# Low weight parts of a first block by ScalarE's negative copy and an accumulating DMA, in place of VectorE's subtraction

## The chip, the cores and the metric

The kernel runs on one core of a Trainium2 chip. The core has five engines with a queue of instructions each, which run in order: TensorE (PE), VectorE (DVE), ScalarE (ACT), GpSimd (POOL) and SyncE (SP). Sixteen DMA engines move data between the HBM and the on-chip memory (SBUF). The metric is device time in microseconds. Before the change the median of two runs is 3559.07 us (3555.22 and 3562.92).

## The reference

Two blocks are computed one after the other, on 512 latent tokens (and 256 context tokens in block 1) of width 2048, all in fp32. Block 1 is one hybrid layer:

```python
u_l = rms_norm(h_lat, pre_w) * (1 + scale_l[:, None]) + shift_l[:, None]
u_c = rms_norm(h_ctx, pre_w) * (1 + scale_c) + shift_c
z_l, xbc_l, dt_l, qkv_l, b_l, a_l = _split_proj(u_l @ w_in)
z_c, xbc_c, dt_c, qkv_c, b_c, a_c = _split_proj(u_c @ w_in)
...
ssd_c, ssd_l = ssd_mixer(xbc_c, dt_c, xbc_l, dt_l, ssd_a_log, ssd_dt_bias, ssd_d)
gdn_c, gdn_l = gdn_mixer(qkv_c, b_c, a_c, qkv_l, b_l, a_l, gdn_a_log, gdn_dt_bias)
...
h_lat = h_lat + gate_l[:, None] * merge(ssd_l, gdn_l, z_l, h_lat.dtype)
```

`scale`, `shift` and `gate` come from a modulation, a vector times a 2048 x 6144 matrix. `ssd_mixer` is a state-space scan, `gdn_mixer` a gated delta rule with a triangular solve in each chunk of 128 tokens; both run forward and backward. `merge` norms both halves, gates them with `silu(z)`, multiplies by `w_out` and norms again. Block 2 has two layers of its own (HGRN2 and RG-LRU, then mLSTM), each with an input projection, an output projection and a gated embedding. The change doesn't reach it.

## The kernel before

Every large product is an fp32 product made of three faster ones. Each operand is split into a high part (the value rounded to the fp32r format of PE) and a low part (the value less its high part), and a product is low x high + high x low + high x high. The parts of the activations (`xh`, `xl`) are made once and stay in SBUF; the parts of the weights are made for each tile, just ahead of their use.

`gemm_steps` (L165) is the line of the products. A weight block is 2048 x 128 and comes in four tiles of 128 partitions x 4 chunks x 128 columns, 256 KB each. For each tile SP loads the raw weights `wr` (L180, four buffers), ScalarE copies them into the high part `wh` (L183), and VectorE subtracts to get the low part `wl` (L184). `wh` and `wl` have six buffers each (`w_bufs`). Then 12 matmuls a stream follow (L198), for each of the four chunks first the one with the low weight part. The three steps of the weights are traced with high priority. Some blocks run over the latent tokens alone (`lat`, 512 columns), others over latent and context (`both`, 512 and 256).

Block 1 goes through these stages:

- Startup (`startup`, L309): 16 steps of the modulation. In each, 2 MB of `wada` come in eight tiles, ScalarE makes the high part (L336), VectorE the low part of six tiles and GpSimd that of two (L337), PE multiplies (L340); then the activations of one contraction chunk are normed, modulated and split (`modulate`, L367). The first four blocks of weights (`w_xbc`, `w_small`) are multiplied chunk by chunk beside it.
- Phase A (`phase_a`, L760): first the SSD, with its blocks of x, B and C, its units of four heads and the first k and v blocks; then the preparation of the gated delta rule, `gdn_prep` (L658) for eight heads, each with loads of decays (`E`, `Rgb`), a first step on GpSimd (L671), transposes and products on PE, stores, and two solves on GpSimd for heads 0 to 3 (`gdn_solve`, L738, L752 and L754).
- Phase B (`phase_b`, L1079): the scans of eight heads, with the remaining 21 blocks (z and queries) woven between the dependent matmuls. PE's order is written out by hand here (`run_slots`, `feed`); the first head's loads are put ahead of the weights on SP.
- `merge` (L1239): output projection, norm, gate, residual.

The startup and phase A are laid out by a planner that simulates the engines (`schedule_with_timeline_sim`, L1898); each engine then keeps the order that it was given. In all, block 1 takes 53 weight blocks ahead of `merge`: 12 of `w_xbc`, 1 of `w_small`, 24 of `w_qkv`, 16 of `w_z`.

Of the kernel before, what the change touches and what calls it, by code (L numbers as in the profile page):

```python
# [17 lines left out]
# products of other blocks between the dependent ones of the gated delta rule, by weight  # L18
# [4 lines left out]
# ---------------------------------------------------------------- layout on the host  # L23
# [107 lines left out]
# ---------------------------------------------------------------- the program  # L131
class Prog:
# [8 lines left out]
    # ---- constants  # L141
# [18 lines left out]
    # ---- products with split operands  # L160
# [4 lines left out]
    def gemm_steps(self, blocks, kc=16):  # L165
        """blocks: dicts of src [128, kc, M], acts [(hi, lo, psum ap)], done().  The blocks run
        together, contraction chunk by contraction chunk; a step is one matmul."""
# [6 lines left out]
        for q in (self.order if kc == 16 else range(kc // qk)):  # L174
            sp = []
            for b in blocks:
                m = b["src"].shape[2]
                with self.tc.high_priority():
                    r = wp.tile([P, qk, m], F32, tag="wr", name="wr", bufs=self.wr_bufs)
                    nc.sync.dma_start(r, b["src"][:, q * qk:(q + 1) * qk, :])  # L180
                    hi = wp.tile([P, qk, m], F32R, tag="wh", name="wh", bufs=self.w_bufs)
                    lo = wp.tile([P, qk, m], F32R, tag="wl", name="wl", bufs=self.w_bufs)
                    nc.scalar.activation(out=hi, in_=r, func=AF.Copy)  # L183
                    nc.vector.tensor_tensor(out=lo, in0=r, in1=hi.bitcast(F32), op=SUB)  # L184
                sp.append((hi, lo))
# [18 lines left out]
    def gemm_tokens(self, src, done):  # L204
        """A product with the tokens in the partitions: src [128, 16, n], done(chunk of tokens, psum)."""
# [22 lines left out]
    def weave(self, steps, n, weight):  # L228
        """Steps of other products to place between dependent matmuls: n of them over the given weight."""
# [11 lines left out]
    def run_slots(self, chain, other=None, skip=0, scale=1.0):  # L241
        """A chain of dependent products; between two of them a link of the other chain and steps of the filler."""
# [24 lines left out]
    # ---- small helpers  # L267
# [13 lines left out]
    def rsqrt_rows(self, acc, n, out, tmp):  # L281
        """out[p, t] = (sum_p acc[p, t] / n + eps) ** -0.5, the same in every partition."""
# [6 lines left out]
        # one table for both  # L289
# [3 lines left out]
        # one step of Newton's method  # L293
# [4 lines left out]
    def transposes(self, ps, dst, srcs):  # L298
        """PE transposes of srcs (each [a, b]) next to each other into one bank, one copy out."""
# [8 lines left out]
    # ---- block 1, phase A: modulation, input projections of both streams, SSD, GDN preparation  # L308
    def startup(self):  # L309
        nc, D = self.nc, self.D  # L310
        self.xh, self.xl, self.ch, self.cl = [], [], [], []
        with self.tc.tile_pool(name="st", bufs=2, side="right") as st:
# [8 lines left out]
            # both vectors' high and low parts, next to each other as stationary columns  # L321
# [33 lines left out]
            def square(k):  # L355
                # the streams wait in the places of their parts
# [24 lines left out]
            # the first modulations run beside the loads of the streams  # L381
# [13 lines left out]
    def conv_consts(self):  # L395
        """Half of the convolutions' taps and bias: silu(x) = (tanh(x / 2) + 1) * (x / 2)."""
# [22 lines left out]
    def conv5(self, ps, is_lat, taps, bias, out, th):  # L419
        """out = silu of the centred convolution of ps."""  # L420
# [20 lines left out]
    def both(self, src, done, share=None):  # L441
        """A block over the latent tokens and over the context."""
# [10 lines left out]
    def conv_block(self, names, j, has_bias, sink):  # L453
        """done() of a block that goes through a convolution; sink(out_lat, out_ctx)."""
# [16 lines left out]
    def small_done(self, ps, pc):  # L471
        """dt, beta and alpha of all tokens (context first): decays and their sums in each chunk."""
        nc, b1 = self.nc, self.b1
        with self.tc.tile_pool(name="sm", bufs=1, side="right") as st:
# [59 lines left out]
            # decay to the chunk's end times dt; minus the decay from the chunk's start  # L534
# [5 lines left out]
    # ---- SSD: units of four heads  # L540
# [3 lines left out]
    def ssd_bc(self, kind, lat, ctx):  # L544
        """B or C of a group: keep the feature-major latent part, B also token-major."""
# [12 lines left out]
    def to_tm(self, dst, lat, ctx, eng="act"):  # L558
        """dst[:, c, :] (token-major chunks) from feature-major latent and context parts."""
# [19 lines left out]
    def ssd_unit(self, u, xt):  # L579
        """Four heads; xt [tokens of a chunk, chunk, 256] holds their x."""  # L580
# [35 lines left out]
        # feature-major, to DRAM  # L616
# [40 lines left out]
    # ---- gated delta rule, preparation: everything that needs k and v alone  # L657
    def gdn_prep(self, h):  # L658
# [23 lines left out]
        # token-major k and its squared norms  # L682
# [19 lines left out]
        # token-major v over the norm of k  # L702
# [8 lines left out]
        # X[j, i] = k_j . k_i with the decay between j and i: forward above, backward below  # L711
# [9 lines left out]
        # its diagonal blocks of 32, rows scaled, lower triangular for both directions  # L721
# [16 lines left out]
    def gdn_solve(self, h, g, eng):  # L738
        """Inverses of the unit lower triangular 32-blocks of two heads, a block in a partition."""
# [6 lines left out]
        # in place: 2 on the diagonal turns the column of a step into its negative  # L746
# [13 lines left out]
    def phase_a(self):  # L760
# [74 lines left out]
        with tc.tile_pool(name="gp", bufs=1, side="right") as self.gp:  # L835
# [18 lines left out]
            # the first queries and gate, while the last preparations end  # L854
# [13 lines left out]
    # ---- gated delta rule: the inverses, the scans  # L868
    def gdn_data(self, h, hd):
        """What the scans of a head need."""  # L870
# [4 lines left out]
    def gdn_load(self, h):  # L875
        """The operands of the products for a head's inverses."""
# [35 lines left out]
    def gdn_merge(self, hd):  # L912
        """W = (I + D X)^-1 of every chunk (forward: upper, backward: lower), from its diagonal
        blocks; both directions share the products."""
# [11 lines left out]
        # 32 -> 64  # L926
# [13 lines left out]
        # 64 -> 128  # L940
# [17 lines left out]
    def gdn_step(self, h, hd, cs, S, tag, last=False):  # L958
        """One chunk of both directions' scans: the corrected values; the next states into S."""
# [47 lines left out]
    def gdn_lat(self, h, hd, qf, before):  # L1007
        """before: what takes the last head's outputs."""
# [11 lines left out]
        # squared norms of q  # L1020
# [34 lines left out]
        # the norms of q and of the outputs, token by token  # L1055
# [15 lines left out]
    def zgate(self, ps, pool, pin=lambda ins: ins):  # L1071
        """2 silu(z)."""
# [6 lines left out]
    def phase_b(self):  # L1079
        nc, tc, D = self.nc, self.tc, self.D  # L1080
        self.yF = self.dr.tile([16, P, 512], F32, name="yF")
        with (tc.tile_pool(name="cq", bufs=1) as self.cv, tc.tile_pool(name="gq", bufs=1, side="right", reuse_waits="tile") as g):
            self.gq = g
            self.pads_lat(self.cv)
            # places: what comes first where the last phase ends early
# [14 lines left out]
            # parity of the block of 32 rows  # L1100
# [24 lines left out]
            def others():  # L1125
                """The products beside the scans, and what follows from them."""
# [16 lines left out]
            with tc.manual_schedule(engines={E.PE}):  # L1143
                # the first head's loads before the weights
# [14 lines left out]
                for h in range(8):  # L1159
                    # the next head's inverses and context beside the latent tokens' scans  # L1160
# [35 lines left out]
    # ---- the streams between the products  # L1196
    def acts(self, order=(0, 1, 2, 3)):
        """New activations, whose chunks are taken up four by four in this order."""
# [3 lines left out]
    def act(self, k, raw, scale=None):  # L1202
        """Contraction chunk k of the next product, in its two parts."""
# [11 lines left out]
    def stage(self, src, n, done, group=4, extra=(), filler=None):  # L1215
        """A product's blocks: the first ones together, so that they keep up with its input."""
# [21 lines left out]
    # ---- block 1: output projection, norm, gate, residual; the per-layer embeddings  # L1238
    def merge(self):  # L1239
# [4 lines left out]
        with tc.tile_pool(name="mp", bufs=1, side="right") as g:  # L1244
            self.act_from(self.yF, (0, 2, 1, 3))
            self.ple_in(g, 1)
            # gate of the modulation
# [19 lines left out]
            # the stream, in the places of the gate's weights  # L1267
# [7 lines left out]
            # some of the embeddings' products run beside the norm  # L1275
# [16 lines left out]
    # ---- per-layer embeddings: projections, their norms; they wait for nothing  # L1292
# [25 lines left out]
    def norm_rows(self, acc, tmp):  # L1318
        """The norm's scale of each token, and half of it."""
# [4 lines left out]
    def columns(self, Rc):  # L1324
        """The norm's scale of each token as columns."""
# [10 lines left out]
    def silu_rows(self, pool, ps, tag, bufs=2, out=None):  # L1336
        """silu of the normed projection."""
# [22 lines left out]
    # ---- even layer  # L1360
    def even(self):
        nc, tc, D = self.nc, self.tc, self.D
        self.yF = self.dr.tile([16, P, 512], F32, name="yF2")
        with tc.tile_pool(name="ep", bufs=1, side="right") as g:
# [7 lines left out]
            # masks of the levels: s in a first half, t in the second half of the same block; and the other way  # L1372
            self.lm, self.lt = {}, {}
            tmp = g.tile([P, 64], F32, name="lmt")
            for m in (64, 32, 16, 8, 4, 2, 1):
# [3 lines left out]
                # 2 m b <= s < 2 m b + m  # L1379
# [7 lines left out]
                # 2 m b + m <= t < 2 m b + 2 m  # L1387
# [576 lines left out]
```

## Time and profile before

| | |
|---|---|
| median of two runs | 3559.07 us |
| span of the profiled execution | 3565.4 us (its own time is not given beside the span) |
| PE busy | 3410.4 us, 96% |
| VectorE busy | 2172.4 us, 61% |
| ScalarE busy | 1511.4 us, 42% |
| GpSimd busy | 543.6 us, 15% |
| share of the 16 DMA engines (the queue that carries the data) | 45.1% |
| read from HBM | 415.17 MB |

Busy time counts the stretch in which an engine has an instruction running; PE's is modelled from pipelined matmuls. Stages are read best from their own stretch, since each has another limit: startup 0 to 205 us, SSD 205 to 550, preparation 550 to 780, scans 780 to 1205, and from there `merge` and block 2.

### The profile page before, as it was taken

What the parts mean: (1) busy time and instruction counts of PE and PEld (TensorE: products, weight loads), DVE (VectorE), ACT (ScalarE), POOL (GpSimd) and SP (SyncE); (2) the same over time, 40 slices, a digit from 0 to 9 for tenths busy, and PEclk for the clock granted to TensorE, in tenths of its full rate; (3) what the DMA queues carried; (4) which work ended last, traced back from release to release, by engine and by line L of the source; (5) the groups of instructions that cost most, each with busy time, mean ns of one, the idle gap of its engine ahead of it and who ended that gap; (6) DMA issues with size and microseconds to landing.
All of it is one profiled execution on the core that took longest, in us unless ns stands there. A gap on an engine that the chain in (4) does not pass through costs nothing.

```text
span 3565.4 us, 49253 instructions
## 1 busy us (share of the span) xinstructions
PE 3410.4 (96%) x17334; PEld 2843.3 (80%) x17334; DVE 2172.4 (61%) x4187; ACT 1511.4 (42%) x3036; POOL 543.6 (15%) x679
## 2 busy tenths in 40 slices
PE   5899999989999998999999999999999999999998
PEld 4688888878888786778888788887888888878887
DVE  7978776778865657666565634546444535353456
ACT  6554434444444435664333434434333333332334
POOL 4211114851110003202231201000000000000000
PEclk8999999999999999999999999999999999999999
DMA  8723336664443774333323454453333333345345
GB/s 272 239 78 108 92 83 215 205 193 133 126 127 94 231 250 137 101 113 95 98 83 98 116 183 136 136 149 107 107 105 101 101 102 102 89 132 156 96 123 170
DMA packets 293257, 479.79 MB, mean 135 GB/s; under 512 B 53689, under 2 KB 86841, under 8 KB 290833
## 3 DMA queue, kind: packets, MB, share of 16 engines
q1 hardware_dynamic: 293008, 476.65, 45.1%
q8 instruction: 136, 2.23, 0.3%
q14 instruction: 113, 0.92, 0.1%
HBM read 415.17 MB, written 61.34 MB: 134 GB/s over the span
## 4 chain that ended last, share of the span: by engine, by line
PE 72%; DVE 12%; DMA 7%; issue 3%; ACT 3%; POOL 2%; SPq 0%; DVEq 0%; ACTq 0%; POOLq 0%
PE mm L198 52%; PE mm L222 3%; PE mm L223 2%; PE mm L224 2%; PE mmc L198 2%; DVE wl L184 2%; DMA wg<-in_wgate 1%; PE pr L340 1%; DVE e L1570 1%; PE mg L922 1%; PE pl L198 1%; DMA araw<-yF 1%; ACT wh L183 1%; DVE at L1577 1%; PE s L198 1%
## 5 line engine op out<-in xcount | busy, mean ns | idle before, releaser
L198 PE MATMUL mm<-hi,wl 128*128 128x512 f32 (+2 forms) x3632 | 1414.7, 392 | 22.7 <-DVE wl L184 14.6
L198 PE MATMUL mm<-xlo,wh 128*128 128x512 f32 (+2 forms) x3632 | 1421.0, 391 | 6.4 <-DVE xlo L278 6.4
L198 PE MATMUL mm<-hi,wh 128*128 128x512 f32 (+2 forms) x3632 | 1415.1, 390 | 0.0
L184 DVE TENSOR_TENSOR wl<-wr,wh 128x512 fp32r<-128x512 f32 (+1 forms) x940 | 657.4, 705 | 687.0 <-ACT wh L183 683.1
L183 ACT ACTIVATE wh<-wr 128x512 fp32r<-128x512 f32 (+1 forms) x940 | 579.6, 621 | 1153.4 <-PE mm L198 908.0
L198 PEld LDWEIGHTS mm<-hi,wl 128*128 128x128 f32 (+1 forms) x3632 | 687.2, 190 | 149.2 <-DVE wl L184 19.9
L198 PEld LDWEIGHTS mm<-xlo,wh 128*128 128x128 f32 (+1 forms) x3632 | 686.6, 189 | 143.0 <-DVE xlo L278 8.7
L198 PEld LDWEIGHTS mm<-hi,wh 128*128 128x128 f32 (+1 forms) x3632 | 686.0, 189 | 122.8 <-issue 3.6
L222 PE MATMUL mm<-wl,hi 128*128 128x256 f32 (+1 forms) x512 | 172.3, 336 | 0.0
L223 PE MATMUL mm<-wh,xlo 128*128 128x256 f32 (+1 forms) x512 | 172.2, 336 | 0.0
L224 PE MATMUL mm<-wh,hi 128*128 128x256 f32 (+1 forms) x512 | 172.0, 336 | 0.0
L216 ACT ACTIVATE wh<-wr 128x512 fp32r<-128x512 f32 x96 | 60.6, 632 | 156.5 <-PE mm L224 77.7
L217 DVE TENSOR_TENSOR wl<-wr,wh 128x512 fp32r<-128x512 f32 x96 | 68.4, 714 | 88.9 <-ACT wh L216 88.4
L436 DVE SCALAR_TENSOR_TENSOR cvl<-padl,hc,cvl 128x512 f32<-128x512 f32 x112 | 91.8, 827 | 24.7 <-ACT cvl L432 15.5
L198 PE MATMUL mmc<-xlo,wh 128*128 128x256 f32 x368 | 106.0, 288 | 0.0
L222 PEld LDWEIGHTS mm<-wl,hi 128*128 128x128 f32 x512 | 97.2, 190 | 10.4 <-DVE pad L1349 0.3
L198 PE MATMUL mmc<-hi,wl 128*128 128x256 f32 x368 | 105.4, 286 | 0.0
L198 PE MATMUL mmc<-hi,wh 128*128 128x256 f32 x368 | 105.3, 286 | 0.0
L223 PEld LDWEIGHTS mm<-wh,xlo 128*128 128x128 f32 x512 | 97.2, 190 | 10.0
L224 PEld LDWEIGHTS mm<-wh,hi 128*128 128x128 f32 x512 | 97.2, 190 | 10.0
L340 PE MATMUL pr<-wal,c 128*4 128x256 f32 x256 | 69.4, 300 | 23.7 <-DVE c L324 10.6
L336 ACT ACTIVATE wah<-wa 128x512 fp32r<-128x512 f32 x128 | 74.5, 620 | 39.7 <-PE pr L340 23.7
(588 smaller groups left out, 4406.1 us busy)
## 6 DMA issues: line engine op xcount, KB each, us to landing
wr<-in_o_in SPq DMA_DIRECT2D x192, 256.0 KB, 3.1
wr<-in_e_in SPq DMA_DIRECT2D x160, 256.0 KB, 3.1
wr<-in_pgate SPq DMA_DIRECT2D x148, 256.0 KB, 3.3
wa<-in_wada SPq DMA_DIRECT2D x128, 256.0 KB, 4.2
wr<-in_w_qkv SPq DMA_DIRECT2D x96, 256.0 KB, 3.2
wr<-in_w_z SPq DMA_DIRECT2D x64, 256.0 KB, 3.1
wr<-in_w_out SPq DMA_DIRECT2D x64, 256.0 KB, 4.5
wg<-in_wgate SPq DMA_DIRECT2D x16, 1024.0 KB, 7.5
```

Of the source, the lines that this page charges most:

```text
L183: nc.scalar.activation(out=hi, in_=r, func=AF.Copy)
L184: nc.vector.tensor_tensor(out=lo, in0=r, in1=hi.bitcast(F32), op=SUB)
L198: nc.tensor.matmul(ap, w[:, kk, :], x, start=(n == 0), stop=(n == total[key] - 1))
L216: nc.scalar.activation(out=hi, in_=r, func=AF.Copy)
L217: nc.vector.tensor_tensor(out=lo, in0=r, in1=hi.bitcast(F32), op=SUB)
L222: nc.tensor.matmul(ps[c][:, :n], self.xh[k][:, t], lo[:, i], start=first, stop=False)
L223: nc.tensor.matmul(ps[c][:, :n], self.xl[k][:, t], hi[:, i], start=False, stop=False)
L224: nc.tensor.matmul(ps[c][:, :n], self.xh[k][:, t], hi[:, i], start=False, stop=last)
L336: nc.scalar.activation(out=wh, in_=w, func=AF.Copy)
L340: nc.tensor.matmul(pr[0:4, 0:256], c4[:, 2 * q + j, :], x[:, j, :], start=(q + j + i == 0), stop=(q + j + i == 9))
L436: nc.vector.scalar_tensor_tensor(out=ov, in0=pad[:, :, j:j + n], scalar=taps[j], in1=ov, op0=MUL, op1=ADD)
L922: nc.tensor.matmul(v[:, c], lhs[:, c], rhs[:, c], start=True, stop=True)
```

## The change

In `gemm_steps` the low part gets a second way. ScalarE copies the raw weights once more with the scale -1 into the tile of the low part, which rounds and leaves minus the high part there; then a DMA issued by GpSimd reads the same weights from HBM again and adds them to that tile. A switch chooses the way: it is on from the start of `run` and goes off ahead of `merge`.

```diff
                     nc.scalar.activation(out=hi, in_=r, func=AF.Copy)
-                    nc.vector.tensor_tensor(out=lo, in0=r, in1=hi.bitcast(F32), op=SUB)
+                    if self.lo_dma:
+
+                        nc.scalar.activation(out=lo, in_=r, func=AF.Copy, scale=-1.0)
+                        nc.gpsimd.dma_start(lo, b["src"][:, q * qk:(q + 1) * qk, :], accum_op=ADD)
+                    else:
+                        nc.vector.tensor_tensor(out=lo, in0=r, in1=hi.bitcast(F32), op=SUB)
...
         self.wr_bufs, self.w_bufs = 4, 6
+        self.lo_dma = True
         self.order = (0, 1, 2, 3)
...
                 self.pq.release()
                 return
+            self.lo_dma = False
             rp = tc.alloc_tile_pool(name="rp", bufs=1)
```

The rest of the diff takes out comments.

## Rows read from the trace of the kernel before

**Rows 1.** The page's totals: busy us, share of the span, instructions.

```profile
span 3565.4 us, 49253 instructions
PE 3410.4 (96%) x17334; PEld 2843.3 (80%) x17334; DVE 2172.4 (61%) x4187; ACT 1511.4 (42%) x3036; POOL 543.6 (15%) x679
```

**Rows 2.** Windows: us, busy PE, PEld, DVE, ACT, POOL, then clock, DMA share, GB/s.

```profile
0.00:60.00 60.00, 24.51 (x122) 13.43 (x122) 43.31 (x68) 43.66 (x84) 29.19 (x34) 0.80 0.90 305
0.00:205.00 205.00, 157.47 (x959) 116.28 (x960) 166.57 (x286) 124.12 (x242) 68.10 (x70) 0.88 0.69 225
205.00:550.00 345.00, 337.75 (x1943) 296.18 (x1943) 275.40 (x624) 144.22 (x316) 48.27 (x56) 0.99 0.35 95
550.00:780.00 230.00, 211.82 (x1181) 183.51 (x1180) 169.57 (x324) 105.15 (x285) 149.18 (x220) 0.96 0.70 215
600.00:750.00 150.00, 135.60 (x761) 118.01 (x760) 119.51 (x216) 61.97 (x170) 126.90 (x179) 0.95 0.65 201
...
780.00:1205.00 425.00, 403.85 (x2357) 345.61 (x2355) 300.35 (x769) 201.48 (x491) 66.23 (x82) 0.99 0.45 130
1205.00:3565.00 2360.00, 2299.54 (x10900) 1901.74 (x10900) 1260.47 (x2187) 936.41 (x1705) 211.80 (x251) 0.99 0.43 125
```

**Rows 3.** PE's waits by stage: SSD, preparation, scans; us in total, times, longest.

```profile
PE yo L595 <- DVE H L614: 4.8, 2, 2.7
...
PE mm L198 <- DVE wl L184: 1.8, 1, 1.8
...
PE og L1046 <- DVE W L925: 3.9, 6, 0.8
```

**Rows 4.** Waits of all engines over the whole span, the longest total.

```profile
ACT wh L183 <- PE mm L198: 908.0, 452, 12.9
```

**Rows 5.** VectorE's subtraction by stage: ns min/median/max, first and last start us.

```profile
L184 DVE TENSOR_TENSOR wl<-wr,wh x18: 674/679/693, 5.1 to 169.0; 128x512 fp32r<-128x512 f32 x18
L184 DVE TENSOR_TENSOR wl<-wr,wh x71: 674/684/719, 208.1 to 545.1; 128x512 fp32r<-128x512 f32 x71
L184 DVE TENSOR_TENSOR wl<-wr,wh x48: 677/693/2144, 552.2 to 779.7; 128x512 fp32r<-128x512 f32 x48
L184 DVE TENSOR_TENSOR wl<-wr,wh x30: 678/804/2144, 602.2 to 748.2; 128x512 fp32r<-128x512 f32 x30
L184 DVE TENSOR_TENSOR wl<-wr,wh x87: 676/693/1520, 779.7 to 1204.4; 128x512 fp32r<-128x512 f32 x87
```

**Rows 6.** Groups by line, 205 to 1205 us: ScalarE's high copy (busy us, mean ns).

```profile
L183 ACT ACTIVATE wh<-wr 128x512 fp32r<-128x512 f32 x207 | 129.3, 628 | 163.5 <-PE mm L198 89.6 <-PE mmc L198 62.3 <-DMA wr<-in_w_z 4.1
```

**Rows 7.** SP's weight loads (L180): issue in ns, and landing.

```profile
L180 SPq DMA_DIRECT2D wr<-in_w_xbc x48: 327/328/437, 0.8 to 411.9; - x48
...
DMA to landing us min/median/max: 2.0/3.2/9.3
```

**Rows 8.** Groups by line on GpSimd, 600 to 750 us.

```profile
L752 POOL TENSOR_TENSOR To<-T 96x31 f32<-96x31 f32 (+15 forms) x62 | 41.6, 671 | 4.2
L754 POOL TENSOR_TENSOR T<-T,To 96x31 f32<-96x31 f32 (+15 forms) x62 | 41.0, 661 | 4.6
L671 POOL TENSOR_SCALAR E<-E,AAg 128x128 f32<-128x128 f32 x36 | 24.8, 706 | 10.7 <-DMA E<-AA 10.7
...
L678 POOL TENSOR_TENSOR vf<-E,mL 128x512 f32<-128x512 f32 x6 | 8.2, 1363 | 0.1
```

**Rows 9.** The chain at the start of the scans: start us, us, what.

```profile
757.17 6.43 DMA wr<-in_w_z
764.28 0.70 DVE wl L184
```

**Rows 10.** The chain in the startup: a load; the first and last wl behind 60 us.

```profile
16.89 4.72 DMA raw<-in_xT
...
84.96 0.60 DVE wl L184
...
165.84 0.60 DVE wl L184
```

## The prediction

> **What bounds the kernel now.** I read the page's totals first, then the busy time of each engine by stage, then the waits, and the chain last. The totals say that PE is busy 96% of a span of 3565.4 us [rows 1]. No time of that execution beside its span is shown; the span stands 6.3 us above the median of the two timed runs, 3559.07, and I add the change in us to the median.
>
> The change touches block 1 alone, that is the time up to about 1205 us; the 2360 us behind it [rows 2] run the same code as before. Within block 1 the bound moves. Up to 205 us (modulation, first four blocks of products) PE is busy 157 of 205 us, VectorE 167, and the DMA engines 69%, in the first 60 us 90%: a start limited by loads and VectorE, PE third. From 205 to 550 (SSD) PE is busy 337.8 of 345, VectorE 275: PE alone is the bound. From 550 to 780 (GDN preparation) PE loses 18 us; within it, from 600 to 750, GpSimd is busy 126.9 of 150. From 780 to 1205 (GDN scans) PE loses 21.2 of 425 [rows 2].
>
> So VectorE is loaded but not what PE waits for. PE waited for a low part (wl) 1.8 us in the preparation, and no longer than that in the other stages [rows 3]; ScalarE instead waited 908 us for PE to give back weight buffers, so the weights are made well ahead [rows 4]. PE's waits for other VectorE work are small pieces, 3.9 us and less in the scans, 4.8 us in the SSD stage [rows 3].
>
> **The change, part by part.** 53 blocks of four weight tiles go through it: 212 tiles, 18 of them made before 205 us, 71 up to 550, 48 up to 780 (30 of these between 600 and 750), and the remaining 75 in the scans; the 87 that the row counts there hold tiles of later products too [rows 5].
>
> *Removed:* 212 subtractions on VectorE, 0.68 to 0.80 us each by the medians [rows 5], about 148 us. Where PE is the bound this is worth nothing. In the scans PE's waits named to VectorE are pieces of 3.9 us and less inside a loss of 21 us [rows 2, 3]; VectorE loses 75 x 0.69 = 52 of 300 busy us, a sixth, and I take -5 us for shorter queues in front of those pieces (ends: 0, and -12).
>
> *Added on ScalarE:* 212 copies like the one that makes the high part, 0.63 us [rows 6], 133 us over 1205. ScalarE would be busy 55 to 66% of each stage (205 to 550: 144 + 71 x 0.63 = 189 of 345); its queue already stops where the high copy waits for PE, and the new copy stands behind the same wait, so what is queued behind it waits 0.63 us longer. I cost this at nothing; without that cover it would be 0.63 us a tile. SP's next load of raw weights is freed by ScalarE's second copy instead of VectorE, at about the same time.
>
> *Added on GpSimd:* 212 DMA issues. GpSimd issues none before, so nothing prices one. SP issues a load of the same tile in 0.33 us [rows 7]; GpSimd's own instructions over 128x512 take 1.36 us [rows 8]. This is work in GpSimd's queue, so I take 1.36, and keep 0.33 as the low end. In the SSD stage 71 x 1.36 = 97 us fit beside 48 busy of 345, in the scans 102 beside 66 of 425 [rows 2]. Between 600 and 750 they don't: 30 x 1.36 = 41 us on top of 126.9 make 168 in 150, **+18 us**; with 0.33 us it would be 137 and nothing. GpSimd runs there the two solves (83 us) and the first step of each preparation [rows 8], and the scans' first operands follow in the same queue, so the overflow pushes the scans' start. An issue also waits for ScalarE's negative copy, which waits for PE: behind it stand solve steps and E rows, a cost I hold in the range, not in the sum.
>
> *Added on the DMA engines:* 212 x 256 KB read again. A plain load costs, at 95 GB/s for a share of 0.35 [rows 2], 0.97 us of all 16 engines. An accumulating one reads its destination too; no row shows one. Low end: 0.97. High end: the dearest plain loads landed in 9.3 us against a median of 3.2 [rows 7], three times, so 2.9 us. I take the low end, as the rows show the engines doing nothing slower than a plain load when they are not crowded. It is harmless in the SSD stage (the share of 0.35 becomes 0.55) and in the scans (0.45 becomes 0.62). In the preparation 0.70 becomes 0.90 [rows 2]: loads on the chain there land later, again kept for the range.
>
> *The longer way to a low part.* Before: high copy, then 0.69 us. After: high copy, 0.63 us, 1.36 us, a landing of 3.2 us at the median [rows 5 to 7], some 5 us more. In the SSD stage a tile lasts 345/71 = 4.9 us, and with six buffers a low part is begun about five tiles, 24 us, ahead; in the scans a tile lasts 5.7 us. Cost: nothing, as long as the way stays below that. There is no lead at two places. At the start of the scans the chain runs from a weight load of 6.4 us through wl straight into the products [rows 9]; the tile then needs 0.63 + 1.36 + 5 (between the median landing and that 6.4) - 0.70 = **+6 us**. In the first stage six of the 18 tiles fall into the first 60 us, where the DMA engines are 90% full and the chain runs through loads [rows 2, 10]: 6 x 0.97 = 5.8 us of transfers in front of the streams, I take +4. Against it, five pieces of wl, about 3 us, stand on that stage's chain behind 60 us [rows 10], of which I give back 2: **+2 us** (ends -8 and +15).
>
> Sum: +2 (start) + 0 (SSD) + 18 (preparation) + 6 (switch) - 5 (scans) = +21 us, 3559 + 21 = **3580 us**.
>
> **Rivals.** *VectorE's relief wins.* A cheap issue (0.33 us) takes away the 18 us; in the preparation 30 x 0.80 = 24 us of VectorE go [rows 5], of which I take 10 on the chain. For it: VectorE is the busiest engine beside PE. Against it: PE's named waits for VectorE are few. By the ends: -8 (start), -10 (preparation), +4 (switch), -12 (scans) = -26 us, 3533. Chance 0.25.
>
> *The transfer counts twice.* It reads the weights and the destination, so two plain loads, 1.94 us a tile. SSD and scans still have room (0.75 and 0.79), the preparation has not: 48 x 1.94 = 93 us in 69 free [rows 2], 24 us more, 3604. The trace has no adding transfer for or against it. Chance 0.12. The Trainium skill (Collectives: The Full Stack, The bandwidth ceiling: the fold count and why AG ≠ RS ≠ AR) states this as a rule: a transfer that adds is slower not for the addition but because it needs two source reads, which halves its rate; no run here shows it yet, and by it the sum would be those 24 us longer.
>
> *The accumulating transfer is dear and becomes the bound.* With a price a per tile, the engines' free time is 64 us in the first stage, 224 in the SSD stage, 69 in the preparation, 234 in the scans [rows 2]. The preparation breaks first, at a = 69/48 = 1.4 us; SSD and scans at 3.2 and 3.1. A 2% loss (71 us) needs a of about 2.9, three plain loads: 48 x 2.9 - 69 = 70. At four plain loads, a = 3.9: 6 + 53 + 118 + 59 = 236 us, so 3795. Nothing in the profile excludes it; for the cheaper price speaks only that plain loads run at 0.97. Chance 0.14.
>
> *It changes nothing that can be seen.* Weight parts are hidden before and stay hidden after: within 5 us, 3559. The planner that lays out the first 750 us lays them out anew, which may move some us either way. Chance 0.11. That the change misses its target I rule out: every product of block 1 up to the scans goes through the changed line, while the output projection stays on VectorE because the switch is set back ahead of it.
>
> **Numbers.** The forecast, +6 to +60 us, has a chance of 0.38. The range goes from 3535, where most of the relief case is in, to 3645, which is the preparation at +41, the first stage at +15, and 30 us for blocked queues and late loads there. What is left out is the dear transfer and the tail of the relief. About 2% (71 us) is what a measurement of this kernel can tell from no change. A gain beyond it is out of reach: PE's losses after 205 us in block 1 add to 7 + 18 + 21 = 46 us [rows 2]. Faster 0.02, same 0.84, slower 0.14.
>
> **What would show it.** VectorE's busy time falls by some 148 us, ScalarE's rises by 133; GpSimd shows 212 issue rows, whose length decides 0.33 against 1.36. The preparation (first row of E to the first scan product) is longer by 18 us, with GpSimd near full; the SSD stage keeps its 345 us. PE's waits name a DMA of wl at the start of the scans and hardly elsewhere. I am wrong if PE waits for DMA wl all through the SSD stage (transfer dear), if the DMA share there goes over 0.8, or if the scans shorten by more than 12 us.

## The result, and the profile after

The changed kernel takes 3659.72 us (median of two runs, 3658.70 to 3660.74) against 3559.07: a ratio of 1.0278, with an interval from 1.0243 to 1.0312. It is slower by about 100 us; the forecast was +21 us, and its range ended 15 us below this. The profiled execution's span grew from 3565.4 to 3659.0 us.

First the page of the changed kernel: the totals, the queues (packets, MB, share of 16 engines), two of the new groups (ScalarE's second copy, and GpSimd's issues for one of the four weight matrices: busy us, mean ns, idle before), and the issues of weights (KB each, us to landing).

```profile
span 3659.0 us, 49560 instructions
...
PE 3427.1 (94%) x17334; PEld 2855.3 (78%) x17334; DVE 2049.6 (56%) x3975; ACT 1624.2 (44%) x3250; POOL 714.4 (20%) x891
...
q1 hardware_dynamic: 293008, 476.65, 43.8%
q0 software_dynamic: 30528, 55.59, 9.0%
...
L186 ACT ACTIVATE wl<-wr 128x512 fp32r<-128x512 f32 x212 | 132.3, 626 | 166.1 <-PE mm L203 86.4
...
L187 POOL DMA_DIRECT2D wl<-in_w_qkv x96 | 84.8, 885 | 191.8 <-ACT wl L186 180.7
...
wr<-in_w_qkv SPq DMA_DIRECT2D x96, 256.0 KB, 4.4
wl<-in_w_qkv POOLq DMA_DIRECT2D x96, 256.0 KB, 5.4
```

Against [rows 1], VectorE is relieved by 122.8 us and 212 instructions, ScalarE has 112.8 us more, GpSimd 170.8 us more. The new queue q0 holds the 212 accumulating transfers: 9.0% of 3659 us is 329 us of all 16 engines, **1.55 us a tile**. An issue stands in GpSimd's record for 0.87 us (the median of all 212; the page gives means), and the transfer lands 5.4 us behind it; the plain loads beside it land in 4.4 us.

The windows of the changed kernel, cut where the same work of before stood in [rows 2] (columns as there), and one stretch of 50 us across the switch to the scans:

```profile
0.00:60.00 60.00, 18.97 (x86) 8.93 (x87) 31.61 (x46) 40.85 (x80) 29.35 (x38) 0.98 0.95 298
0.00:220.00 220.00, 157.88 (x964) 114.16 (x964) 157.90 (x267) 132.07 (x262) 89.90 (x90) 0.95 0.76 231
220.00:578.00 358.00, 341.30 (x1941) 296.82 (x1940) 237.98 (x553) 184.25 (x390) 104.86 (x125) 0.99 0.65 144
578.00:855.00 277.00, 216.57 (x1207) 187.04 (x1206) 137.19 (x277) 131.20 (x337) 180.45 (x269) 0.90 0.83 225
855.00:1300.00 445.00, 411.14 (x2327) 354.59 (x2326) 254.82 (x690) 239.03 (x558) 127.30 (x156) 0.95 0.69 168
1300.00:3659.00 2359.00, 2300.18 (x10903) 1902.72 (x10901) 1261.68 (x2189) 937.60 (x1708) 211.94 (x251) 0.99 0.43 125
...
800.00:850.00 50.00, 15.91 (x72) 13.37 (x73) 6.77 (x16) 16.46 (x38) 29.19 (x62) 0.62 0.66 180
```

Each stage lasts longer for the same PE work (the start 220 us for 205, the preparation 277 for 230), and the rest of the kernel lasts as long as before, 2359 us. In the last row PE works 15.9 of 50 us, at a granted clock of 0.62 in the mean of the stretch.

PE's waits in the first 1320 us of the changed kernel (total us, times, longest):

```profile
PE mm L203 <- DMA wl<-in_w_z: 36.4, 1, 36.4
PE vT L309 <- DMA vf<-vD: 16.8, 4, 10.4
...
PE mg L927 <- DVE rS L975: 13.9, 6, 2.8
...
PE mm L203 <- DMA wl<-in_w_xbc: 6.5, 3, 2.6
```

One wait of 36.4 us is over a third of the loss: the first products beside the scans wait for their low part. The chain of the changed kernel (start us, us, what) tells what that low part waited for:

```profile
814.30 1.27 POOL T L760
815.93 1.35 POOL W L896 x2
817.28 1.36 POOL X L1099 x2
...
825.34 2.78 issue
828.13 5.91 DMA wl<-in_w_z
834.09 6.31 PE mm L203 x16
```

The second solve ends on GpSimd at 815.6 us, the memsets and the scans' first operands follow in the same queue, and only then, at 828.1, the transfer starts. Before, the first raw weights of the scans were loaded from 757.2 on, and VectorE made the low part right behind them [rows 9].

How late the work is was worked out from the two traces: each matmul of the changed kernel against the same matmul of before, as the median of 20 us at five marks of before's time (behind the start, at the end of the SSD stage, ahead of and behind the switch to the scans, behind the scans). In us:

| kernel | start (210) | SSD (540) | prep. (735) | switch (780) | scans (1300) |
|---|---|---|---|---|---|
| the change | 14.6 | 27.5 | 34.7 | 75.6 | 94.1 |
| copy by ScalarE, addition by VectorE | 4.0 | 8.1 | 12.4 | 15.1 | 35.0 |
| DMA of 8 KB | -5.3 | -0.7 | 1.3 | 29.1 | 38.4 |
| change in the scans only | 3.3 | 3.3 | 3.0 | 16.5 | 43.7 |
| second solve on VectorE | 16.7 | 27.5 | 34.0 | 64.6 | 89.3 |
| both solves on VectorE | 14.4 | 27.6 | 34.6 | 47.4 | 66.0 |
| negative copy by VectorE | 10.5 | 27.6 | 36.0 | 61.3 | 100.2 |
| accumulation beside | 10.4 | 49.9 | 62.6 | 95.5 | 142.1 |
| plain load beside | -1.2 | 9.7 | 15.2 | 41.4 | 61.1 |
| 8 KB, both solves on VectorE | 1.4 | 3.6 | -4.0 | -0.6 | 2.2 |
| 8 KB beside | 8.2 | 19.3 | 26.5 | 50.7 | 59.3 |
| before, both solves on VectorE | -1.1 | -0.3 | -5.3 | -3.3 | -7.1 |
| plain load, both solves on VectorE | 6.6 | 9.5 | 6.6 | 13.3 | 26.3 |

So the loss of the change is +15 in the start, +13 in SSD, +7 in the preparation, +41 at the switch, +19 in the scans. A single profile's marks move by some us (the control row ends at -7 where its timed runs show -4), so steps of 5 us and less are not argued from. Some of these executions also lie off the median of their kernel's runs: 8 KB beside by 15 us above it, the plain load with both solves by 9 and the change in the scans only by 8, the two DMAs of 8 KB into the low part by 5 and 6 us below; the losses that these rows give are off by as much in all.

### The profile page after: what moved, and what is told of

It reads as the page before. It is cut to its first block, busy times and chain, and to the rows that moved or that the text cites. A ratio compares the mean times of both kernels' runs of the same rounds, so it can differ in the third digit from the quotient of the medians.

```text
span 3659.0 us, 49560 instructions
## 1 busy us (share of the span) xinstructions
PE 3427.1 (94%) x17334; PEld 2855.3 (78%) x17334; DVE 2049.6 (56%) x3975; ACT 1624.2 (44%) x3250; POOL 714.4 (20%) x891
## 3 DMA queue, kind: packets, MB, share of 16 engines
q0 software_dynamic: 30528, 55.59, 9.0%
## 4 chain that ended last, share of the span: by engine, by line
PE 70%; DVE 12%; DMA 8%; ACT 4%; issue 4%; POOL 3%; SPq 0%; ACTq 0%; DVEq 0%; POOLq 0%
PE mm L203 52%; PE mm L227 2%; PE mm L228 2%; PE mm L229 2%; PE mmc L203 2%; DMA Rf<-AA 1%; PE mg L927 1%; DVE wl L189 1%; DVE e L1575 1%; PE pl L203 1%; DMA qe<-EA 1%; DVE cvl L441 1%; DMA wl<-in_w_small 1%; ACT wh L183 1%; DMA araw<-yF 1%
## 5 line engine op out<-in xcount | busy, mean ns | idle before, releaser
L203 PE MATMUL mm<-hi,wl 128*128 128x512 f32 (+2 forms) x3632 | 1420.2, 393 | 63.8 <-DMA wl<-in_w_z 36.4
L189 DVE TENSOR_TENSOR wl<-wr,wh 128x512 fp32r<-128x512 f32 (+1 forms) x728 | 502.9, 698 | 622.1 <-ACT wh L183 619.1
L186 ACT ACTIVATE wl<-wr 128x512 fp32r<-128x512 f32 x212 | 132.3, 626 | 166.1 <-PE mm L203 86.4
L187 POOL DMA_DIRECT2D wl<-in_w_qkv x96 | 84.8, 885 | 191.8 <-ACT wl L186 180.7
L227 PEld LDWEIGHTS mm<-wl,hi 128*128 128x128 f32 x512 | 97.2, 190 | 10.5 <-DVE pad L1354 0.3
```

Source lines behind the costliest of these rows:

```text
L186: nc.scalar.activation(out=lo, in_=r, func=AF.Copy, scale=-1.0)
L187: nc.gpsimd.dma_start(lo, b["src"][:, q * qk:(q + 1) * qk, :], accum_op=ADD)
L203: nc.tensor.matmul(ap, w[:, kk, :], x, start=(n == 0), stop=(n == total[key] - 1))
L227: nc.tensor.matmul(ps[c][:, :n], self.xh[k][:, t], lo[:, i], start=first, stop=False)
```

## The experiments

Two theories stood at first. A: the accumulating DMA (its traffic and its queue on GpSimd) makes the loss. B: ScalarE's second copy of every tile makes it. Diffs are against the changed kernel, unless said otherwise; ratios are against before on the same chip.

**Copy by ScalarE, addition by VectorE.** No DMA is added.

```diff
-                        nc.gpsimd.dma_start(lo, b["src"][:, q * qk:(q + 1) * qk, :], accum_op=ADD)
+                        nc.vector.tensor_tensor(out=lo, in0=r, in1=lo.bitcast(F32), op=ADD)
```

> ScalarE still makes the negative copy for the 212 tiles of block 1, but VectorE adds the raw weights to it instead of the DMA: the added ScalarE work alone, without GpSimd issues and without transfers. Theory A (the transfers on the DMA engines and the issues in GpSimd's queue are the loss): 3550 to 3575 us, ScalarE busy 133 us more than before, VectorE as before. Theory B (ScalarE's second copy, queued behind PE's release of the buffers, delays the other work on ScalarE): at least 20 us of the 100 stay, 3580 us or more.

3600.8 us, 1.0097 [1.0082, 1.0113]. By itself this spoke for B (3580 us or more) for a third of the loss, 20 of the 35 us in the scans. It proves less than it seemed: VectorE is not relieved here and stands behind two copies instead of one.

**DMA of 8 KB.** The transfer is cut from 256 to 8 KB, the issues and the wait stay.

```diff
-                        nc.gpsimd.dma_start(lo, b["src"][:, q * qk:(q + 1) * qk, :], accum_op=ADD)
+                        nc.gpsimd.dma_start(lo[:, 0, 0:16], b["src"][:, q * qk, 0:16], accum_op=ADD)
```

> As the change, but the accumulating DMA adds only 16 columns of one of the tile's four chunks, 8 KB in place of 256, in as many rows; the rest of the low part is left as minus the high part. All 212 issues on GpSimd stay, the traffic goes. Theory A1 (traffic on the DMA engines makes the loads of each stage land later): the losses of startup, SSD stage and scans (15 + 12 + 27 us) go, what stays is the stall ahead of the scans (about 35 us): 3585 to 3610 us, and loads of qe and Yf land in 4.5 us again. Theory A2 (the order of GpSimd's queue is the loss): 3640 us or more.

3611.0 us, 1.0123 [1.0108, 1.0138], a little above theory A1's range: the scans still lose 9 us, though qe and Yf land in 4.4 us, as that theory has it. Without the other 248 KB, the start and the SSD stage lose nothing: those 27 us come with the bytes, by the traffic or by the later landing of the low part itself (5.5 us at the median in the change, 3.5 here), which this kernel doesn't tell apart. The stall at the switch stays, PE's longest wait in this kernel:

```profile
PE mm L203 <- ACT wh L183: 28.6, 1, 28.6
```

**Change in the scans only.**

```diff
-        self.lo_dma = True
+        self.lo_dma = False
...
             self.rw = tc.alloc_tile_pool(name="rw", bufs=1)
+            self.lo_dma = True
             self.phase_b()
```

> The accumulating DMA only in the scans: startup, SSD and preparation make the low parts on VectorE as before, with the layout of before. Theory A1 (traffic): the scans lose some 3.5 us a head as in the changed kernel, 25 to 30 us, and a few us at their start: 3585 to 3600 us. Theory A2 (GpSimd's queue): the first low parts of the scans stand behind no solve steps now, since the solves end at 747 us as before; the stall of 36 us goes, and little else is lost: 3560 to 3575 us.

3601.3 us, 1.0102 [1.0086, 1.0119], just above theory A1's range and far above that of A2. The first two stages stand as before (+3 us); the switch still costs 13 us and the scans 27, more than the 19 they cost in the full change.

**Second solve on VectorE.**

```diff
-                    self.gdn_solve(2, self.gp, nc.gpsimd)
+                    self.gdn_solve(2, self.gp, nc.vector)
```

> The change, with the second solve (heads 2 and 3) on VectorE instead of GpSimd. Theory A2 for the start of the scans (the first low parts are issued by GpSimd only when the second solve and the operands behind it are through, 798 to 828 us, and PE stands for 36 us): that wait shrinks to under 8 us and the time falls by 25 to 35 us, to 3625 to 3635. Rival (the wait is that of transfers landing late, or of PE's own order): less than 10 us is gained, 3650 or more.

3654.7 us, 1.0252 [1.0235, 1.0269]: a miss: 5 us less by the medians and 9 by the ratios, where 25 to 35 were expected, so the rival's range (3650 or more). The stall fell from 36.4 to 24.8 us only. The trace of the changed kernel says why. GpSimd's waits from 560 to 820 us (total, times, longest), and a piece of its queue inside the first solve (start us, us, line, in brackets the idle time before):

```profile
POOL wl L187 <- ACT wl L186: 34.5, 14, 5.3
```

```profile
713.21 0.98 POOL L759 TENSOR_TENSOR T<-T,To 96x240 f32<-96x240 f32 x1
714.26 0.61 POOL L757 TENSOR_TENSOR To<-T 96x231 f32<-96x231 f32 x1
716.70 0.89 POOL L187 DMA_DIRECT2D wl<-in_w_qkv  x1 [1.83 <-ACT cvc L437]
717.33 0.94 POOL L759 TENSOR_TENSOR T<-T,To 96x231 f32<-96x231 f32 x1
...
720.92 0.89 POOL L187 DMA_DIRECT2D wl<-in_w_qkv  x1
721.53 0.90 POOL L759 TENSOR_TENSOR T<-T,To 96x207 f32<-96x207 f32 x1
```

The issues stand ahead of the solves and between their steps, in program order: from 560 to 820 us there are 42 of them, whose records add to 37.9 us. The records of neighbours overlap, and the next instruction starts some 0.63 us behind an issue's start (the rows above; the median where nothing was waited for), so that an estimate of the time they take from the queue is 42 x 0.63 = 26 us. And 14 of them hold the queue for another 34.5 us because ScalarE has not made its copy yet, 24 us of it ahead of the first solve. The first and the last step of that solve, before and in the changed kernel (its last row gives the first and last start of four solves):

```profile
606.74 0.16 POOL L747 MEMSET T<- 96x32 f32 x1 [0.40 <-DMA T<-LX]
...
L755 POOL TENSOR_SCALAR_AFFINE_SELECT T<-T x4: 1262/1280/1610, 676.3 to 942.3; 96x1024 f32<-96x1024 f32 x4
```

```profile
646.93 0.16 POOL L752 MEMSET T<- 96x32 f32 x1 [4.46 <-DMA T<-LX]
...
L760 POOL TENSOR_SCALAR_AFFINE_SELECT T<-T x4: 1267/1270/1270, 749.1 to 982.2; 96x1024 f32<-96x1024 f32 x4
```

It starts 40 us late, where PE's work is some 28 late, and lasts 102 us instead of 70; what stands behind it on GpSimd, the preparation's own steps that the second solve needs among them, waits as long. Moving the second solve alone leaves that.

**Both solves on VectorE.** The line above, and the same edit in `gdn_solve(0, ...)`.

> Both triangular solves of the preparation run on VectorE instead of GpSimd; the changed kernel otherwise. Theory P: the stall at the start of the scans (36.4 us) is made in GpSimd's queue, where from 560 to 820 us 35 DMA issues take 31.6 us and wait 34.5 us more for ScalarE's negative copies, with the 124 steps of the two solves behind them; the second solve ends 66 us late (747 to 815). With the solves elsewhere the stall falls under 8 us, the second solve ends before 780 us, and the kernel takes 3615 to 3635 us. Rival V: VectorE, which holds the convolutions in order, gets 83 us more work in the same stretch, or the loads and stores of the preparation are what is late; then the stall stays over 15 us and the kernel takes 3640 to 3665 us.

3633.9 us, 1.0194 [1.0172, 1.0216]. (The count of issues in the expectation, 35 and 31.6 us, is that of 640 to 840 us.) The stall is gone, as theory P says; PE's wait for the same weights in this kernel:

```profile
PE mm L203 <- DMA wl<-in_w_z: 5.8, 1, 5.8
```

The switch falls from 41 to 13 us late, the other stages keep their losses to the microsecond (14, 13, 7, 19). GpSimd's queue, with the solves in it, costs 26 to 30 us; 66 of the 94 are something else.

**Negative copy by VectorE.**

```diff
-                        nc.scalar.activation(out=lo, in_=r, func=AF.Copy, scale=-1.0)
+                        nc.vector.tensor_scalar(out=lo, in0=r, scalar1=-1.0, scalar2=None, op0=MUL)
```

> The negative copy is made by VectorE in place of ScalarE; the accumulating DMA stays. ScalarE is then as loaded as before the change and VectorE too, and the time against before is that of the DMA and of its wait alone. Theory B (ScalarE's second copy of 0.63 us costs some 35 us, 25 of them in the scans, as the kernel with copy and VectorE addition showed): 3615 to 3640 us, the scans lose under 10 us. Theory A (transfers and the longer way to the low part make up nearly all by themselves, and the two costs overlap rather than add): 3645 to 3670 us, the scans lose 20 us or more.

3670.8 us, 1.0310 [1.0293, 1.0327]. With ScalarE as loaded as before the change, the time gets worse, not better. Theory B falls: the second copy on ScalarE is not what the change pays for. The scans lose 39 us here, twice what they lose in the change; why is open.

**Accumulation beside, plain load beside.** VectorE subtracts as before; the transfer goes to the raw tile, which nobody reads any more.

```diff
-                        nc.scalar.activation(out=lo, in_=r, func=AF.Copy, scale=-1.0)
-                        nc.gpsimd.dma_start(lo, b["src"][:, q * qk:(q + 1) * qk, :], accum_op=ADD)
+                        nc.vector.tensor_tensor(out=lo, in0=r, in1=hi.bitcast(F32), op=SUB)
+                        nc.gpsimd.dma_start(r, b["src"][:, q * qk:(q + 1) * qk, :], accum_op=ADD)
```

The second kernel has the last line without `accum_op`.

> VectorE makes the low parts as before; the same accumulating DMA adds the weights onto the raw tile, which nobody reads any more, so that nothing but the tile's reuse waits for it. Left over is the traffic and the 212 issues in GpSimd's queue. Theory A (traffic and queue): 3600 to 3640 us, of it +12 to +17 in the start and +8 to +14 in the SSD stage. Theory C (the time lies in the wait of the products for the low part, not in the traffic): 3566 to 3585 us.

> As the kernel before this one in the series, but the second transfer loads the weights again instead of adding them: same bytes from the weights, same issues, no accumulation. If accumulating costs 1.55 us of all 16 DMA engines for a tile against 0.88 us of a plain load, the start (18 tiles, DMA at 0.99) is 10 to 14 us shorter than with accumulation, and the kernel 12 to 30 us shorter. If accumulating is no dearer than loading, the two are within 5 us.

3704.4 us, 1.0396 [1.0378, 1.0414], and 3630.6 us, 1.0197 [1.0182, 1.0212]. The first is above the range expected: the raw tiles stay taken until the transfer lands, so SP's loads start later (up to 600 us they wait 265 us in 68 waits for these transfers), which the expectation had not priced. Between the two, where only the addition differs, lie 74 us, over twice what was expected; the longer hold of the raw tiles may be a part of that. The queue's line on the page of the accumulating kernel, then of the plain one:

```profile
q0 software_dynamic: 30528, 55.59, 9.1%
```

```profile
q0 software_dynamic: 16960, 55.59, 5.2%
...
L187 POOL DMA_DIRECT2D wr<-in_w_qkv x96 | 54.5, 568 | 214.2 <-DVE wl L186 159.8
```

The same bytes take 0.091 x 3705.6 / 212 = 1.59 us of all engines a tile with the addition, and 0.052 x 3625.7 / 212 = 0.89 without; the record of an issue is 0.57 us without and 0.89 with it (means of the groups of `in_w_qkv`).

**8 KB, both solves on VectorE.**

> Both solves on VectorE and the accumulating DMA cut to 16 columns (8 KB of 256; the low part is otherwise left as the negative copy). Left of the change are ScalarE's copy, the 212 issues and the wait for a short transfer. Theory P (the stall at the start of the scans is GpSimd's queue): the 28.6 us stall of the kernel with the short DMA goes, and the kernel stands at -5 to +8 us at the start of the scans and at 3570 to 3590 us in the end, the rest being the scans' own +11. Rival V (the stall has another cause): the stall stays above 15 us and the time at 3595 to 3615 us.

3572.4 us, 1.0034 [1.0020, 1.0049], inside theory P's range. ScalarE's 212 copies, 212 issues, the wait and a landing of 3.6 us at the median all remain, and cost 12 us. PE's wait for the weights at the switch, in this kernel:

```profile
PE mm L203 <- DMA wl<-in_w_z: 5.3, 1, 5.3
```

**8 KB beside.** As accumulation beside, with `r[:, 0, 0:16]` and 16 columns of weights.

> VectorE makes the low parts as before; the GpSimd queue adds only 16 columns (8 KB) onto the raw tile that nobody reads. Left over are the 212 issues in GpSimd's queue and the wait of each for VectorE, with no traffic, no second copy of ScalarE, and no product that waits. Theory P: the switch to the scans is 15 to 30 us late by the queue alone, the other stages lie within 5 us of before, and the time is 3580 to 3600 us. If the scans' loss of 11 us without traffic is ScalarE's second copy, the scans add under 4 us here; if it is GpSimd's queue, they add 8 to 14. Rival: issues alone cost nothing, and the stall came from ScalarE's queue: 3560 to 3572 us.

3611.0 us, 1.0136 [1.0119, 1.0153], above the range expected. The switch is 24 us late by the queue alone, as theory P says; GpSimd's wait from 560 to 820 us, and PE's at the switch:

```profile
POOL wr L187 <- DVE wl L186: 34.5, 17, 6.2
```

```profile
PE mm L203 <- DVE wl L186: 24.5, 1, 24.5
```

Two things missed: the start and the SSD stage, expected within 5 us, are 8 and 11 us late, though hardly a byte is moved. There a raw tile is held until GpSimd has issued and the transfer has landed, and SP's loads wait for that. SP's longest wait before (0 to 550 us), then the two longest here (0 to 570 us):

```profile
SPq L180 <- DVE wl L184: 136.2, 56, 7.5
```

```profile
SPq L180 <- DMA wr<-in_w_qkv: 125.6, 34, 9.0
SPq L180 <- DMA wr<-in_w_xbc: 115.0, 33, 8.8
```

That this makes the 8 and 11 us was not tried by itself, and the profiled execution is one of 15 us above the median. The scans add 9 us.

**Before, both solves on VectorE.** The two edits of the solves on the kernel before the change.

> The kernel before the change, with both solves of the preparation on VectorE instead of GpSimd: the control of the two kernels that had the solves there. If moving the solves gains or costs nothing by itself (83 us more on VectorE, which is busy 200 to 230 of 300 us there), 3555 to 3575 us, and what the solves gave back to the changed kernel (26 and 38 us) was GpSimd's queue alone. If VectorE becomes the bound of the preparation, 3580 to 3610 us, and the queue of GpSimd has cost the changed kernel more than the two differences show. If the solves on GpSimd already bounded the kernel before, 3535 to 3553 us: then it beats both kernels, and a part of the two differences is that gain.

3556.8 us, 0.9991 [0.9981, 1.0000]. Moving the solves is free in the kernel before (within 7 us, by the interval), so what it gave back to the changed one was the queue.

**Plain load, both solves on VectorE.** The kernel with both solves moved, without `accum_op`.

> The changed kernel with both solves on VectorE, and the second transfer a plain load of the weights over the negative copy instead of an accumulation (the low part is then the weights themselves). Same bytes of weights, same issues, waits and order as the kernel with accumulation and both solves on VectorE (3633.9 us); with 8 KB in place of 256 the same kernel took 3572.4 us. If the price is the accumulation's dear transfer (1.55 us of all 16 engines a tile against 0.88 for a load), the 61 us between these two shrink to under 30: 3570 to 3600 us, qe and Yf land in about 5 us in the scans, and the start is less than 5 us late. If any second transfer of the weights costs this, accumulating or not: 3615 to 3640 us.

3583.6 us, 1.0056 [1.0039, 1.0074]. The queue's line in this kernel:

```profile
q0 software_dynamic: 30528, 55.59, 6.0%
```

That is 1.02 us a tile. A second full read of the weights costs 8 us over the 8 KB, which is as much as the intervals leave open; making it an accumulation costs 50 us more. The scans' landings (qe and Yf, 860 to 1240 us) stand at 4.8 and 5.0 us, yet the scans lose 13 us; the start is 6.6 us late, a little over the 5 expected.

No version beats the kernel before; the nearest, with the solves moved and no DMA at all, equals it.

## Why the prediction was wrong

Two steps failed. The transfers were priced as plain loads (0.97 us a tile, measured 1.55) and called harmless in the SSD stage and in the scans, since the mean share of the DMA engines left room; as additions they cost some 49 us, those of the start included. And the wait that an issue brings into GpSimd's queue was held "in the range, not in the sum"; with the issues it cost some 30 us, paid at the switch to the scans.

The runs with both solves moved split the loss, in parts of before's time, by the difference of ratios (the ratios have intervals of 0.0014 to 0.0022 to either side, the change's own 0.0034, so that the four parts are known to some 15, 10, 8 and 5 us, and the third is not clear of zero):

| part | ratios | us |
|---|---|---|
| GpSimd's queue, with solves and issues in it | 1.0278 - 1.0194 | 30 |
| the addition: an accumulating transfer for a plain one | 1.0194 - 1.0056 | 49 |
| a plain second load for 8 KB | 1.0056 - 1.0034 | 8 |
| ScalarE's copy, the issues, the longer way | 1.0034 - 1 | 12 |

The other order gives the same within that: shortening the DMA with the solves on GpSimd saves 1.0278 - 1.0123, 55 us, and moving the solves then 32.

*The price of the transfer: wrong, and the largest part.* The step "I take the low end, as the rows show the engines doing nothing slower than a plain load" set 0.97 us, and the change measures 1.55. The plain load is where it was put (0.89 and 1.02). The rival that was weighed beside this, two loads a tile, was the better guide: against a plain load an addition takes 1.54 / 1.02 = 1.5 times as long into the tile of the low part (both with the solves moved) and 1.59 / 0.89 = 1.8 times into the raw tile. With two loads a tile the forecast would have been 3604, still 56 us short. The Trainium skill (Collectives: The Full Stack, The bandwidth ceiling: the fold count and why AG ≠ RS ≠ AR) has such a rule for the ReduceScatter of a collective, where the two source reads of an add halve the rate. The trace agrees with it in kind and falls short of the factor of two, at 1.5 and 1.8.

*The step from share to time: wrong too.* The forecast held added traffic harmless wherever the DMA engines' mean share left room, and let it cost only beyond that. At a = 1.55 its own formula for the preparation gives 48 x 1.55 - 69 = 5 us, and nothing for SSD and scans. The SSD stage lost 13 us at a share of 0.65, below the 0.8 named as the sign, and the scans 19 at 0.69. The other sign, PE waiting for a DMA of wl all through the SSD stage, stayed away too: from 220 to 578 us none of PE's waits names one. What grew there is the landing of other loads that stand on the chain. The broadcast rows of the SSD stage, before (210 to 550 us) and after (220 to 578):

```profile
Rf<-AA SPq DMA_DIRECT2D x16, 256.0 KB, 4.0
```

```profile
Rf<-AA SPq DMA_DIRECT2D x16, 256.0 KB, 5.3
```

and the loads of the scans, before (780 to 1205) and after (855 to 1300):

```profile
qe<-EA SPq DMA_DIRECT2D x16, 256.0 KB, 4.5
Yf<-ED SPq DMA_DIRECT2D x8, 256.0 KB, 4.4
```

```profile
qe<-EA SPq DMA_DIRECT2D x14, 256.0 KB, 6.7
Yf<-ED SPq DMA_DIRECT2D x7, 256.0 KB, 6.1
```

Two us a head, with eight heads in a row, is the size of the scans' loss; in the kernel with 8 KB and moved solves they land in 4.1 and 4.5 us and the scans add 3. But this is not shown to be the cause, and other runs speak against its being all: with the plain load and moved solves they land only 0.3 to 0.6 us later than before and the scans lose 13 us (in an execution 9 us above the median), and with copy and addition by VectorE they land in 4.5 and 4.3 us and the scans lose 20. Some 7 of the 19 us lie in PE's own busy time, 411.1 us against 403.9, at a mean granted clock of 0.95 against 0.99 [rows 2]. What makes up the scans' loss stays open.

*The start: +2 forecast, +15 measured,* at the far end that was kept for it. The form of that term, six transfers in front of the streams, fits; its price was too low. All six issues start before 16 us, and at 20 us PE's work is 8.9 us late (matched as in the table of marks), where 6 x 1.55 is 9.3. With the plain load and moved solves it is 5.5, where 6 x 1.02 is 6.1; with 8 KB and moved solves 1.2, where 6 x 0.25 is 1.5. A load on the chain there, before and after (start us, us, what):

```profile
10.44 6.43 DMA wa<-in_wada
```

```profile
11.26 14.05 DMA wa<-in_wada
```

Another 7 us come on between 60 and 200 us, where the forecast gave 2 back for five pieces of wl on the chain [rows 10]. In the changed kernel the chain goes there through three landings of wl:

```profile
91.96 9.29 DMA wl<-in_w_small
...
134.99 8.90 DMA wl<-in_w_small
...
179.63 9.97 DMA wl<-in_w_small
```

That the landings make these 7 us is not shown: with 8 KB and moved solves the chain has three of 6.7 to 7.8 us there, and that stretch loses nothing.

*GpSimd's issues: 1.36 us taken, 0.87 measured,* of which some 0.63 keep the next instruction waiting. The mechanism was right, GpSimd's queue overflowing between 600 us and the scans; its size came from elsewhere. The clause "behind it stand solve steps and E rows, a cost I hold in the range, not in the sum" is the step that failed here: 14 waits of 34.5 us in all, more than the 26 us that the 42 issues themselves take from the queue from 560 to 820 us. And the loss was looked for in the preparation (+18, measured +7) instead of at its end: PE went on with products that don't need the solves, and paid at the switch, +41 where +6 stood. The sign named for it, a wait for a DMA of wl at the start of the scans, is there, at 36.4 us.

*ScalarE's copy, costed at nothing: right as far as it can be told,* at most the 12 us of the last part. Why copy and addition in series lose 20 us in the scans without any added transfer is open.

*VectorE's relief, -5 us:* not seen in the change. The 122.8 us that VectorE lost (148 were forecast) bought nothing that PE waited for, as the first section of the prediction had it.

## What to carry to other kernels

An operation put into an engine's queue brings its wait along, and everything behind it in program order inherits that wait; price the wait before the operation, and look for the loss where the delayed work is next needed. Don't take the mean share of the DMA engines as room: here loads on the chain landed a third to a half later at shares of 0.65 and 0.69. An accumulating DMA is to be priced as more than a load, 1.5 to 1.8 times here, before it replaces a cheap vector operation that nobody waits for.

## What the runs showed of the hardware

An accumulating DMA of 8 KB is far from free: 1.5% of 3566 us for 212 of them is 0.25 us of all engines each, in 144 packets a transfer (30528 / 212), as many as for the 256 KB. A plain load of 256 KB takes 144 packets too into the fp32r tile of the low part, and 80 (16960 / 212) into the raw tile. GpSimd's record of an issue is 0.87 us long for an accumulating transfer and 0.54 to 0.55 for a plain one of the same tile (medians), where SP's is 0.33 [rows 7]; the next instruction on GpSimd starts 0.62 to 0.64 us behind the start of an accumulating issue and 0.60 us behind that of a plain one, where it waits for nothing else.
